# Seven half-size products in place of eight for the gate and up projections of two feed-forwards

## The chip, the core and the metric

The kernel runs on one core of a Trainium2 chip. The metric is the device time of one execution in microseconds, the median of several runs. Inputs and outputs are fp32. Engines are named as in the profile: PE is TensorE's matmul, PEld its weight load, DVE VectorE, ACT ScalarE, POOL GpSimd, SP the engine that issues the DMAs.

## What is computed

Two layers of a first block, each a mixer of four kinds of heads and a feed-forward, and then two attention layers of a second block, over 512 tokens of width 1024. The change touches the two feed-forwards alone. Of one, the reference computes (h is the normalised x):

```python
def conv_glu_ffn(h, w_gate, w_up, conv_w, w_down):
    gate = causal_dwconv(h @ w_gate, conv_w)      # 3 taps along the tokens, per column
    return (jax.nn.gelu(gate, approximate=True) * (h @ w_up)) @ w_down
# w_gate, w_up: 1024 x 2816; w_down: 2816 x 1024
# x = x + rms_norm(conv_glu_ffn(rms_norm(x, pre_ffn_g[l]), ...), post_ffn_g[l])
```

## The kernel before

**Precision.** A product in fp32 is made of three matmuls in fp32r: each operand is split into hi (a cast on ScalarE) and lo = source - hi (a subtraction on VectorE, or on GpSimd where eng says so); `mm3` issues hi x hi, hi x lo and lo x hi into the same PSUM tile.

**Weights.** `wload` takes a buffer wr (two of them, 4 KB a partition each), loads 512 KB from HBM by SP, and splits it into wh and wl (four buffers each). `preload` does the same for a view that comes later.

**Gate and up.** A feed-forward has NF = 22 tiles f of 128 columns of w_gate and as many of w_up. For each, `fm` runs 8 blocks of 128 rows x 3 matmuls = 24 matmuls of 512 columns (the tokens) into one PSUM tile psA. Behind each f: a scaled copy out of PSUM on ScalarE, two steps of the convolution on VectorE (gate read from PSUM), a gelu on ScalarE, the multiplication by the up tile, and the split of the result, which stays in SBUF in the form that the down projection reads. The first three tiles run in halves of 256 tokens (`fm_first`), so that they can start on tokens 0 to 255 while the norm of the others is still made. `next_norm` normalises the four blocks of 128 tokens as the projection before delivers them, and `trans_split` transposes each in 8 transposes and splits it out of PSUM.

**Down.** `out_proj` multiplies the activations by w_down, in two halves of 512 columns; a step is two f: 4 token blocks x 2 x 3 = 24 matmuls of 512 columns, into four PSUM tiles. Then `residual_norm` makes the norm and adds x. `then` names the weights that are preloaded before the last of these.

**Order.** Program order is not the order on the engines. Every instruction goes into a planner (`Plan`), which simulates the five engines with costs written in it, gives out instructions by their rank in program order as they become ready and as buffers are free, and then emits one static order; each engine runs its instructions in that order. wr, wh and wl are taken strictly in turn. In the planner's costs the engines do not slow one another.

Every instruction is recorded at one line (L328, the helper that hands it to the planner), so rows are told apart by tiles: psA, psS and psD are the PSUM pools; p4h, p4p and p4w are pools of 4 KB tiles with 8, 8 and 16 buffers; p is a pool of ten 2 KB tiles; st are small ones; xd is x in HBM.

## Time and profile before

| | before |
|---|---|
| median of 3 runs | 2045.97 us (2045.56 to 2046.21) |
| profiled execution | 2043.82 us, span 2042.0 us |
| TensorE busy | 96% of the span |
| VectorE, ScalarE, GpSimd busy | 62%, 47%, 17% |
| TensorE's granted clock, mean | 0.989 |
| DMA | 94 GB/s mean |

The span goes from the first to the last instruction. Busy shares are averages over stages with different limits, so what an engine is worth has to be read from the windows of a stage. A row of a timeline merges neighbouring instructions of one kind; its duration then reaches from the first start to the last end. Spans of GpSimd are rough, so the ends of instructions on other engines beside them are the better measure.

### The profile page before, as it was taken

The numbers are of one execution on the slowest core, as the hardware profiler recorded it, in microseconds if no ns is written. First come the engines' busy times: TensorE is split into PE (matmuls) and PEld (weight loads), VectorE is DVE, ScalarE is ACT, GpSimd is POOL, SyncE is SP. The second block draws the span as 40 slices with busy tenths as digits, with TensorE's granted clock in tenths as the row PEclk, the third lists the DMA queues.
The fourth block names the chain that finished last, engine by engine and source line by source line (L and its number), as shares of the span: only waits on it lengthen the run. The fifth ranks groups of instructions, "written<-read, shape, count | busy, mean of one in ns | idle before, by whom it ended". The sixth has DMA issues, their size and how long they took to land.

```text
span 2042.0 us, 33217 instructions
## 1 busy us (share of the span) xinstructions
PE 1963.9 (96%) x13254; PEld 1663.4 (81%) x13254; DVE 1265.9 (62%) x2313; ACT 955.0 (47%) x1721; POOL 356.8 (17%) x403
## 2 busy tenths in 40 slices
PE   6999999999999999999999999999999999999999
PEld 5888778888888878787788888888899988888787
DVE  7697883644442266879836444422548886558796
ACT  5763363433332246633634333322446663457782
POOL 3312121100000023112203000000323331105131
PEclk9999999999999999999999999999999999999999
DMA  5321224433332433301344333325331213331121
GB/s 159 99 71 36 71 67 164 117 100 93 94 102 93 155 108 93 76 23 55 94 150 119 93 94 102 93 93 175 114 83 49 77 62 114 126 91 53 62 73 62
DMA packets 231305, 191.88 MB, mean 94 GB/s; under 512 B 22224, under 2 KB 201072, under 8 KB 231152
## 3 DMA queue, kind: packets, MB, share of 16 engines
q1 hardware_dynamic: 231152, 189.77, 30.4%
q8 instruction: 104, 1.70, 0.4%
q14 instruction: 49, 0.40, 0.1%
HBM read 174.54 MB, written 15.20 MB: 93 GB/s over the span
## 4 chain that ended last, share of the span: by engine, by line
PE 80%; DVE 11%; ACT 3%; issue 2%; POOL 2%; DMA 1%; SPq 1%; DVEq 0%; ACTq 0%; POOLq 0%
PE psA L328 59%; PE psS L328 12%; PE psD L328 9%; DVE p4w L328 7%; DVE wl L328 1%; POOL st L328 1%; DVE p L328 1%; DVE st L328 1%; ACT p4w L328 1%; DVE p4p L328 1%; SPq L328 1%; ACT wh L328 1%; DVE p4h L328 0%; DMA p4p<-in_x_dram 0%; ACT p L328 0%
## 5 line engine op out<-in xcount | busy, mean ns | idle before, releaser
L328 PE MATMUL psA<-p4h,wh 128*128 128x512 f32 (+1 forms) x2144 | 626.0, 376 | 4.0 <-ACT p4h L328 2.6
L328 DVE TENSOR_TENSOR wl<-wr,wh 128x1024 fp32r<-128x1024 f32 (+5 forms) x290 | 336.6, 1165 | 392.2 <-ACT wh L328 386.8
L328 ACT CAST wh<-wr 128x1024 fp32r<-128x1024 f32 (+6 forms) x304 | 299.0, 990 | 474.8 <-PE psA L328 283.8
L328 PEld LDWEIGHTS psA<-p4h,wh 128*128 128x128 f32 x2144 | 392.6, 190 | 83.2 <-ACT p4h L328 4.4
L328 PE MATMUL psA<-p4h,wl 128*128 128x512 f32 (+1 forms) x1072 | 403.2, 377 | 1.5 <-DVE wl L328 1.5
L328 PE MATMUL psA<-wh,p4h 128*128 128x256 f32 (+1 forms) x1792 | 353.0, 290 | 2.1 <-DVE p4h L328 1.7
L328 PEld LDWEIGHTS psA<-wh,p4h 128*128 128x128 f32 x1792 | 284.0, 190 | 6.6 <-DVE p4h L328 2.3
L328 PE MATMUL psA<-wl,p4h 128*128 128x256 f32 (+1 forms) x896 | 259.8, 290 | 0.0
L328 POOL TENSOR_SCALAR st<-st 128x1 f32<-128x1 f32 (+4 forms) x108 | 40.0, 370 | 1139.1 <-ACT p4w L328 781.4
L328 PEld LDWEIGHTS psA<-p4h,wl 128*128 128x128 f32 x1072 | 203.9, 190 | 35.5 <-DVE wl L328 1.7
L328 PEld LDWEIGHTS psA<-wl,p4h 128*128 128x128 f32 x896 | 170.5, 190 | 1.6
L328 PE MATMUL psA<-wh,p4w 128*128 128x512 f32 (+1 forms) x540 | 159.5, 368 | 0.0
L328 ACT ACTIVATE p<-p 128x512 f32<-128x512 f32 (+2 forms) x174 | 88.1, 526 | 107.1 <-DVE p L328 105.9
L328 POOL TENSOR_TENSOR st<-st,c 128x1 f32<-128x1 f32 (+4 forms) x106 | 113.9, 1077 | 7.5
L328 PEld LDWEIGHTS psA<-wh,p4w 128*128 128x128 f32 x540 | 96.5, 188 | 18.4 <-issue 0.7
L328 ACT ACTIVATE p4w<-psA 128x256 f32<-128x256 f32 (+5 forms) x138 | 61.6, 451 | 101.9 <-PE psA L328 100.9
L328 PE MATMUL psS<-p4w,p4w 128*64 128x64 f32 (+9 forms) x800 | 98.1, 283 | 7.4 <-DVE p4w L328 7.3
L328 PE MATMUL psS<-consts,p4w 128*128 128x128 f32 (+1 forms) x448 | 71.0, 293 | 34.4 <-DVE p4w L328 18.8
L328 PE MATMUL psA<-wl,p4w 128*128 128x512 f32 (+1 forms) x270 | 98.4, 365 | 0.0
L328 PE MATMUL psS<-wh,p4w 128*128 128x512 f32 x300 | 97.4, 395 | 0.0
L328 DVE TENSOR_TENSOR p<-psA,p 128x512 f32<-128x512 f32 x54 | 37.3, 690 | 95.7 <-PE psA L328 94.2
L328 PEld LDWEIGHTS psS<-consts,p4w 128*128 128x128 f32 x448 | 55.1, 154 | 44.4 <-DVE p4w L328 17.1
(228 smaller groups left out, 3242.5 us busy)
## 6 DMA issues: line engine op xcount, KB each, us to landing
wr<-in_w_in_dram SPq DMA_DIRECT2D x44, 512.0 KB, 3.8
wr<-in_ffn_w_gate_dram SPq DMA_DIRECT2D x44, 512.0 KB, 3.8
wr<-in_ffn_w_up_dram SPq DMA_DIRECT2D x44, 512.0 KB, 3.9
wr<-in_ffn_w_down_dram SPq DMA_DIRECT2D x44, 512.0 KB, 3.5
wr<-in_w_out_dram SPq DMA_DIRECT2D x16, 512.0 KB, 4.4
wr<-in_a_w_in_dram SPq DMA_DIRECT2D x16, 512.0 KB, 3.8
wr<-in_b_w_in_dram SPq DMA_DIRECT2D x16, 512.0 KB, 3.9
p4w<-xd SPq DMA_DIRECT2D x12, 512.0 KB, 4.8
```

The lines of the kernel that those rows point to most:

```text
L328: op.fn(*op.args, **op.kw)
```

## The change

For 256 columns (p) of w_gate or w_up, called one n, the weights are seen as 2 x 2 blocks B of 512 rows x 128 columns, the activations as 2 x 2 blocks A of 256 tokens x 512 rows, and the four products of 256 tokens x 128 columns are put together from seven block products in place of eight (Winograd's form). The sums of blocks of activations (s1 to s4) are made once in each feed-forward, in `norm_blocks`, by VectorE and GpSimd before the transposes, and are then transposed and split as blocks of their own. The sums of blocks of weights (t1 to t4) are made for every n by `seven_weights`, in three stages that the loop calls one n ahead: both halves of the raw weights sit in the two wr buffers; GpSimd subtracts (four times 128x512, two of them in place in wr); ScalarE and VectorE split. A product is 12 matmuls of 256 columns. The seven products are added up by VectorE out of PSUM into an SBUF tile u; the convolution and the gelu work on that tile, and GpSimd multiplies by the up half. The activations are kept in fp32 and split later, by `lhs`, while the down projection runs. The lead-in (`lead`) prepares all of the first n and the first stage of the second before the feed-forward begins. PSUM pools of the projection before are used in another order.

```diff
         return h, rest
 
+    def trans4(self, src, blk, t):
+        ps = self.ps("S")
+        for k in range(4):
+            self.tr(ps[:, k * 128:(k + 1) * 128], src[:, k * 128:(k + 1) * 128])
+        self.split(*(b[:, :, t * 128:(t + 1) * 128] for b in blk), ps.rearrange("p (k n) -> p k n", k=4))
+    def norm_blocks(self, steps, grow):
+        gb = self.bcast_row(grow, D)
+        blk, xns = {}, []
+        lo, hi = slice(0, 512), slice(512, 1024)
+        def put(key, src, t, tag):
+            if key not in blk:
+                blk[key] = [self.p4([128, 4, 256], F32R, tag) for _ in range(2)]
+            self.trans4(src, blk[key], t)
+        for t, _ in enumerate(steps):
+            xn = self.p4()
+            self.norm_tok(self.xt[t], gb, xn)
+            xns.append(xn)
+            if t >= 2:
+                put("a11", xns[t - 2][:, lo], t - 2, "h")
+                put("a12", xns[t - 2][:, hi], t - 2, "h")
+        def rest():
+            for j in range(2):
+                x, y = xns[j], xns[2 + j]
+                s1, s2, s3, s4 = (self.p2() for _ in range(4))
+                self.add(s1, y[:, lo], y[:, hi])
+                self.sub(s2, s1, x[:, lo])
+                self.sub(s3, x[:, lo], y[:, lo], self.G)
+                self.sub(s4, x[:, hi], s2)
+                put("s2", s2, j, "p")
+                put("s1", s1, j, "h")
+                put("s3", s3, j, "p")
+                put("s4", s4, j, "p")
+                put("a22", y[:, hi], j, "h")
+        return blk, rest
+    def seven_weights(self, W, c0, out):
+        raw = [self.new(self.pwr, 2, [128, 4, 256], F32, "wr", "wr") for _ in range(2)]
+        for i in range(2):
+            self.SP.dma_start(out=raw[i], in_=self.cols(W, c0, 256)[:, i * 4:i * 4 + 4])
+        b = [[raw[i][:, :, j * 128:(j + 1) * 128] for j in range(2)] for i in range(2)]
+        pair = lambda: [self.new(p, 4, [128, 2, 4, 128], F32R, tag, tag) for p, tag in ((self.pwh, "wh"), (self.pwl, "wl"))]
+        hi, lo = pair()
+        for i in range(2):
+            self.split(hi[:, i], lo[:, i], b[i][0], eng=self.G if out.get("pool") else None)
+        out["b11"], out["b21"] = ((hi[:, i], lo[:, i]) for i in range(2))
+        yield
+        hi, lo = pair()
+        t = self.p4([128, 2, 4, 128])
+        self.sub(t[:, 1], b[0][1], b[0][0], self.G)
+        self.sub(t[:, 0], b[1][1], t[:, 1], self.G)
+        self.split(hi, lo, t)
+        out["t2"], out["t1"] = ((hi[:, i], lo[:, i]) for i in range(2))
+        self.sub(b[1][0], b[1][0], t[:, 0], self.G)
+        self.sub(b[0][1], b[1][1], b[0][1], self.G)
+        yield
+        hi, lo = pair()
+        d = self.p4([128, 2, 4, 128], F32R, "p")
+        self.split(hi[:, 0], lo[:, 0], b[0][1])
+        self.split(hi[:, 1], lo[:, 1], b[1][1])
+        self.split(d[:, 0], d[:, 1], b[1][0], eng=out.get("eng"))
+        out["t3"], out["b22"] = ((hi[:, i], lo[:, i]) for i in range(2))
+        out["t4"] = d[:, 0], d[:, 1]
+        yield
+    def product(self, ps, blk, w):
+        for k in range(4):
+            self.mm3(ps, (w[0][:, k, :], w[1][:, k, :]), (blk[0][:, k, :], blk[1][:, k, :]), k == 0, k == 3)
     def hp(self, h, k, c0, c1):
         return h[0][k // 2][:, k % 2, c0:c1], h[1][k // 2][:, k % 2, c0:c1]
 
@@ -1853,46 +1931,102 @@
             for n, w in hold:
                 part(ps1, t, n, w)
             if t == NT - 1:
-                self.preload(*then, eng=self.G)
+                then() if callable(then) else self.preload(*then, eng=self.G)
             done(t, [ps0[t], ps1[t]])
             yield t
 
-    def ffn_views(self, l):
+    def ffn_weights(self, l):
         I = self.I
-        return [self.cols(I[k][l], f * 128, 128) for f in range(NF) for k in ("ffn_w_gate", "ffn_w_up")]
-
-    def ffn(self, l, h, rest, then):
+        outs = [{"eng": (self.G, None)[n % 2]} for n in range(NF)]
+        gens = [self.seven_weights(I[k][l], p * 256, outs[2 * p + i]) for p in range(NF // 2)
+                for i, k in enumerate(("ffn_w_gate", "ffn_w_up"))]
+        def lead():
+            outs[0]["pool"] = True
+            for i in (0, 0, 0, 1):
+                next(gens[i])
+        return outs, gens, lead
+    def ffn(self, l, blk, rest, weights, then):
 
         I = self.I
         Wd = I["ffn_w_down"][l]
-        views = self.ffn_views(l) + [self.out_rows(Wd, 0, 0)]
-        acts = []
-        first = self.fm_first(h, [self.wload(v) for v in views[:3]], rest)
-        self.preload(views[3])
-
-        def proj(i):
-            if i < 3:
-                return first[i]
-            w = self.wload(views[i])
-            self.preload(views[i + 1])
-            return self.fm(h, w)
-
-        for f in range(NF):
-            psg, psu = proj(2 * f), proj(2 * f + 1)
-            c = self.p2()
-            self.act(c, psg, AF.Copy, scale=self.fcols[l](f, 2))
-            for j in (1, 0):
-                s = 2 - j
-                self.stt(c[:, s:], psg[:, :S - s], self.fcols[l](f, j), c[:, s:], ALU.mult, ALU.add)
-            self.act(c, c, AF.Gelu_apprx_tanh)
-            self.mul(c, psu, c)
-            a = self.p4([128, 2, S], F32R, "w" if f < 16 else "p")
-            self.split(a[:, 0, :], a[:, 1, :], c)
-            acts.append(a)
-        gb = self.bcast_row(I["post_ffn_g"][l], D)
-        self.xt = self.load_x(acts[NF - 1][:, 0, :].bitcast(F32), "w")
-        return self.out_proj(Wd, lambda k, t: (acts[k][:, 0, t * 128:(t + 1) * 128], acts[k][:, 1, t * 128:(t + 1) * 128]),
-                             list(range(0, NF, 2)), lambda t, ps: self.residual_norm(t, ps, gb, "w"),
+        outs, gens, _ = weights
+        acts, tiles, conv = [], {}, []
+        lo, hi = slice(0, 256), slice(256, 512)
+        def head(n):
+            w, u = outs[n], self.p4([128, 4, 256])
+            ps = self.ps("A")
+            self.product(ps[:, lo], blk["a11"], w["b11"])
+            self.product(ps[:, hi], blk["a12"], w["b21"])
+            self.act(u[:, 3], ps[:, lo], AF.Copy)
+            self.add(u[:, 0], ps[:, hi], u[:, 3])
+            tiles[n] = u
+        def more(n):
+            if n < len(gens):
+                next(gens[n])
+            elif n == NF:
+                self.preload(self.out_rows(Wd, 0, 0))
+        head(0)
+        head(1)
+        rest()
+        for n in range(NF):
+            if n >= 2:
+                head(n)
+            w, u = outs[n], tiles.pop(n)
+            more(n + 1)
+            ps = self.ps("D")
+            self.product(ps[:, lo], blk["s2"], w["t2"])
+            self.add(u[:, 3], ps[:, lo], u[:, 3])
+            ps = self.ps("S")
+            self.product(ps[:, hi], blk["s1"], w["t1"])
+            if n + 1 < NF:
+                more(n + 1)
+            self.product(ps[:, lo], blk["s3"], w["t3"])
+            two = lambda a: a.rearrange("p (a n) -> p a n", a=2)
+            self.add(u[:, 1:3], two(ps), u[:, 3:4].broadcast_to([128, 2, 256]))
+            self.add(u[:, 3], ps[:, hi], u[:, 1])
+            ps = self.ps("A")
+            self.product(ps[:, hi], blk["s4"], w["b22"])
+            if n + 2 < NF:
+                more(n + 2)
+            self.product(ps[:, lo], blk["a22"], w["t4"])
+            self.add(u[:, 1:3], two(ps), u[:, 1:3])
+            if n % 2 == 0:
+                conv = []
+                for i in range(2):
+                    g = u[:, 2 * i:2 * i + 2].rearrange("p a n -> p (a n)")
+                    c = self.p2()
+                    conv.append(c)
+                    self.act(c, g, AF.Copy, scale=self.fcols[l](n + i, 2))
+                    for j in (1, 0):
+                        s = 2 - j
+                        self.stt(c[:, s:], g[:, :S - s], self.fcols[l](n + i, j), c[:, s:], ALU.mult, ALU.add)
+                    self.act(c, c, AF.Gelu_apprx_tanh)
+                continue
+            u = u.rearrange("p (f a) n -> p f (a n)", f=2)
+            for i in range(2):
+                self.mul(u[:, i], u[:, i], conv[i], self.G)
+            acts.append(u)
+        gb = self.bcast_row(I["post_ffn_g"][l], D, "p")
+        parts, self.xt = {}, None
+        def lhs(k, t):
+            for p in range(k // 2, min(k // 2 + 2, NF // 2)):
+                if p not in parts:
+                    parts[p] = [self.p4([128, 2, S], F32R, tag) for tag in ("h" if p < 7 else "p", "w")]
+                    self.split(*parts[p], acts[p])
+            if (k, t) == (NF - 1, NT - 1) and not self.xt:
+                self.xt = self.load_x(parts[k // 2][1][:, 0, :].bitcast(F32), "w")
+            return tuple(a[:, k % 2, t * 128:(t + 1) * 128] for a in parts[k // 2])
+        return self.out_proj(Wd, lhs, list(range(0, NF, 2)), lambda t, ps: self.residual_norm(t, ps, gb, "w"),
                              "SSSD", "AAAD", then)
 
     def layer1(self, l, steps):
@@ -1912,17 +2046,18 @@
         mla = self.mla_items(l, W, h, TC)
         mem = self.mem_items(l)
         self.merge(self.project(gdn + gate_d + hgrn + gla + mla + gate_a + gate_b + mem))
+        weights = self.ffn_weights(l)
         gb = self.bcast_row(I["post_mix_g"][l], D)
         mt = self.mixT
         self.xt = self.load_x(mt[3][:, 0, :].bitcast(F32), "p")
         steps = self.out_proj(Wo, lambda k, t: (mt[k][:, 0, t * 128:(t + 1) * 128], mt[k][:, 1, t * 128:(t + 1) * 128]),
-                              order, lambda t, ps: self.residual_norm(t, ps, gb, "p"), "AAAD", "SSSD",
-                              self.ffn_views(l)[:3])
+                              order, lambda t, ps: self.residual_norm(t, ps, gb, "p"), "DAAA", "DSSS",
+                              weights[2])
         if self.upto == f"mix{l}":
             return run(steps)
-        h, rest = self.next_norm(steps, I["pre_ffn_g"][l], "h")
+        blk, rest = self.norm_blocks(steps, I["pre_ffn_g"][l])
         then = self.gdn_views(1, I["w_in"][1])[:2] if l == 0 else self.a_views()
-        return self.ffn(l, h, rest, then)
+        return self.ffn(l, blk, rest, weights, then)
 
 
```

## Rows read from the trace of the kernel before

**Rows 1.** The page: busy us (share of the span) xinstructions.
```profile
PE 1963.9 (96%) x13254; PEld 1663.4 (81%) x13254; DVE 1265.9 (62%) x2313; ACT 955.0 (47%) x1721; POOL 356.8 (17%) x403
```

**Rows 2.** Busy us by windows: PE, PEld, DVE, ACT, POOL, granted clock, DMA, GB/s.
```profile
400.00:450.00 50.00, 50.00 (x220) 41.03 (x219) 24.49 (x29) 18.13 (x24) 0.00 (x0) 1.00 0.33 95
650.00:700.00 50.00, 50.00 (x216) 40.29 (x215) 12.48 (x14) 10.12 (x11) 0.19 (x1) 1.00 0.47 157
...
366.74:370.99 4.25, 4.25 (x21) 4.25 (x21) 4.25 (x6) 2.00 (x2) 1.55 (x1) 0.50 0.73 185
```

**Rows 3.** The chain that ended last, feed-forwards: start, duration, what.
```profile
379.29 233.63 PE psA L328 x1053
612.93 4.20 PE psS L328 x18
617.13 1.40 PE psD L328 x6
```

**Rows 4.** Timeline of VectorE, 1st and 18th: start, duration, instruction [idle before].
```profile
404.29 0.69 DVE L328 TENSOR_TENSOR p<-psA,p 128x512 f32<-128x512 f32 x1 [2.05 <-PE psA L328]
...
591.06 0.69 DVE L328 TENSOR_TENSOR p<-psA,p 128x512 f32<-128x512 f32 x1 [2.04 <-PE psA L328]
```

**Rows 5.** Timeline of TensorE at a feed-forward's start.
```profile
363.92 0.73 PE L328 MATMUL psS<-consts,p4w 128*128 128x128 f32 x4 [3.81 <-DVE p4h L328]
...
377.49 1.04 PE L328 MATMUL psS<-consts,p4w 128*128 128x128 f32 x8
...
379.87 0.28 PE L328 MATMUL psA<-p4h,wl 128*128 128x256 f32 x1
...
381.99 0.28 PE L328 MATMUL psA<-p4h,wl 128*128 128x256 f32 x1
```

**Rows 6.** Timeline of VectorE and GpSimd where both work: early, and before a feed-forward.
```profile
19.36 2.17 POOL L328 TENSOR_SCALAR p<-consts 128x512 f32<-128x512 f32 x1
20.09 1.64 DVE L328 SCALAR_TENSOR_TENSOR p4w<-p4p,st,p4w 128x1024 f32<-128x1024 f32 x1
...
352.27 1.28 DVE L328 TENSOR_TENSOR p4p<-p4p,p4p 128x512 f32<-128x512 f32 x2
...
357.42 2.40 POOL L328 TENSOR_TENSOR wl<-wr,wh 128x1024 fp32r<-128x1024 f32 x1
358.09 0.74 DVE L328 SCALAR_TENSOR_TENSOR p4p<-psS,st,p4w 128x512 f32<-128x512 f32 x1
358.75 1.62 DVE L328 TENSOR_TENSOR p4p<-p4p,p4p 128x512 f32<-128x512 f32 x1
359.77 2.79 POOL L328 TENSOR_TENSOR wl<-wr,wh 128x1024 fp32r<-128x1024 f32 x1
360.29 2.82 DVE L328 TENSOR_TENSOR p4p<-p4p,p4p 128x512 f32<-128x512 f32 x1
```

**Rows 7.** Groups by form, 410 to 590 us: count | busy us, mean ns | idle before.
```profile
L328 DVE TENSOR_TENSOR wl<-wr,wh 128x1024 fp32r<-128x1024 f32 x33 | 40.4, 1225 | 63.7 <-ACT wh L328 62.2
L328 ACT CAST wh<-wr 128x1024 fp32r<-128x1024 f32 x33 | 34.7, 1052 | 81.5 <-PE psA L328 81.5
...
L328 DVE TENSOR_TENSOR p<-psA,p 128x512 f32<-128x512 f32 x16 | 11.1, 691 | 32.7 <-PE psA L328 32.7
...
L328 DVE TENSOR_TENSOR p4w<-p,p4w 128x512 fp32r<-128x512 f32 x13 | 8.9, 683 | 0.0
L328 ACT ACTIVATE p4w<-p 128x512 fp32r<-128x512 f32 x13 | 8.2, 633 | 0.0
```

**Rows 8.** Instructions on wr, 136.5 to 139 us: issue ns, starts, landing.
```profile
L328 SPq DMA_DIRECT2D wr<-in_w_in_dram x2: 395/404/413, 137.2 to 137.7; - x2
...
DMA to landing us min/median/max: 3.4/3.6/3.9
```

**Rows 9.** Timeline of VectorE at the same start.
```profile
376.02 1.28 DVE L328 SCALAR_TENSOR_TENSOR p4w<-p4p,st,p4w 128x1024 f32<-128x1024 f32 x1
377.21 0.42 DVE L328 TENSOR_TENSOR p4h<-psS,p4h 128x256 fp32r<-128x256 f32 x1
```

## The prediction

> **What bounds the kernel now.** I read the page first, then the windows of a feed-forward, then the chain that ended last, then the groups by form, and at the end single pieces of the timeline. The page shows TensorE at 96% of the span and GpSimd at 17% [rows 1]. In a feed-forward TensorE is busy for the whole of each window at the full granted clock, VectorE for about half of it, and GpSimd does next to nothing [rows 2]. The chain agrees: one unbroken TensorE piece of 233.63 us is the gate and up projections of the first layer, and behind it comes the down projection in steps of 4.20 us [rows 3]; the second layer repeats it. So in this stretch nothing but fewer or shorter matmuls can save time, as long as the other engines keep up, and the reader should look for the engine that would not.
>
> The pace of today: the first and the last of 18 multiplications by an up tile start at 404.29 and 591.06 us [rows 4], 17 periods of 10.99 us. A period is one f (a gate and an up tile of 128 columns), 48 matmuls of 512 columns at 229 ns. I call "one n" what the change works on at a time: 256 columns of one of the two matrices, which cost the same 48 matmuls, 10.99 us. There are 22 n in a layer and 44 in all.
>
> **TensorE's share.** An n becomes seven products of 12 matmuls with 256 columns: 84. The trace has such matmuls in the first three projections: at full clock a wl matmul, every third one, stands at 379.87 and another at 381.99, 18 matmuls later [rows 5], so 118 ns each and 1.41 us a product. An n is then 7 x 1.41 = 9.89 us. The gain offered is 1.10 us an n, 48 us in all. Seven eighths would offer more; 256 columns cost slightly over half of 512.
>
> **VectorE and GpSimd, and the port between them.** The weights of an n, two raw halves of 512 KB, now go through four subtractions of 128x512 on GpSimd, a split of 1024 elements and five of 512 (hi on ScalarE, lo = source - hi). The last of these lo parts is on GpSimd for every second n. Each second n also has two products of 128x512 on GpSimd. These now run all through a stretch where GpSimd was idle, and the trace shows what it does to VectorE. An addition p4p<-p4p,p4p with both inputs in SBUF takes 0.64 us (two in 1.28). Issued at 358.75 while GpSimd ran a wl subtraction, it took 1.62 and ended 0.55 after it. The next one, issued at 360.29 under GpSimd's second, took 2.82 and again ended just behind it [rows 6]. GpSimd's second took 2.79 where the first took 2.40: it had waited for VectorE. The scalar_tensor_tensor just before, with one input in PSUM, was not drawn out, 0.74. One with both inputs in SBUF suffers too: 1.64 at 20.09, behind a GpSimd instruction. So an instruction of VectorE with two SBUF inputs and one of GpSimd take turns, whole instruction by whole instruction.
>
> The Trainium skill says so too ("SBUF — State Buffer", section "SBUF: two separate sides"): the pair of ports that both engines share is a lock, and the later one waits for the end of the other's instruction. By that rule the two engines' durations add up; if they shared a rate instead, the additions at 358.75 and 360.29 would have been slowed by the same factor rather than ended where GpSimd did. The trace sides with the rule; without it the second rival below, 2043 us, would be the forecast.
>
> The durations, as the time the port is taken: GpSimd 128x512 is at least 1.07 (the two additions that waited ended at 360.37 and 363.11, 2.74 apart; less one addition's 0.60 leaves 2.14 for 1024), at most 1.20 (half of 2.40) [rows 6]. I take the middle, 1.13. VectorE: 0.60 for 512 (1.28 less the 0.68 that one shows), 1.15 for 1024 (1.225 recorded [rows 7], less the same 0.08), about 0.65 for a scalar_tensor_tensor of 512 from SBUF (a 1024 one shows 1.28 [rows 9], 0.05 over a subtraction).
>
> For two n (one gate, one up):
> - GpSimd: 8 subtractions, 1 lo part, 2 products: 11 x 1.13 = 12.4 us (11.8 to 13.2).
> - VectorE with two SBUF inputs: 9 lo parts of 512 (5.4), 2 of 1024 (2.3), and the 4 convolution steps (2.6), which now read the assembled tile in SBUF where they read PSUM: 10.3 us.
> - Sum on the port 22.7 us (22.1 to 23.5), that is 11.35 an n. TensorE wants 9.89 and the kernel before takes 10.99.
>
> VectorE's additions from PSUM (3 of 256 at 0.42 and 2 of 512 at 0.69 an n [rows 7, 9]) and ScalarE's casts (4.2 us an n from 0.63 and 1.05 [rows 7]) don't take the port; both engines alone would fit (VectorE 15.5 and ScalarE about 12 us for two n).
>
> **The raw buffers.** wr has two buffers, and both halves of one n fill them; before, each held a whole tile's weights and came free after one cast and one subtraction. SP issues the next load when that subtraction ends. Now a half is held until the last splits that read it. From the landing of the second half, in turns on the port: subtraction 1.13, lo of b21 0.60, subtraction 1.13 (it overwrites b21), lo of t 1.15, subtraction 1.13, lo of b22 0.60, lo of t4 1.13 or 0.60, lo of t3 0.60: 7.2 us, 0.3 for hand-overs. Two loads of weights issued 0.5 apart landed 3.4 and 3.9 us after their issue [rows 8]: 4.4 us to the second. Round trip 11.9 us. In the 4.4 us of loading the port is free for the convolution and the products, 2.4 us an n. VectorE's 2.6 us of PSUM additions fall between the links; for an eighth of them to delay one I add 0.3. One n then takes 12.2 us: 1.2 above today, 44 x 1.2 = +53 us. TensorE then idles 2.3 us an n. Bounds: a perfectly packed port, 11.05 (44 x 0.06 = +3 us); half the PSUM additions and the other port work in the way, 13.4 (+106 us).
>
> **Start of a feed-forward, twice.** Before, TensorE stood 3.81 us at 363.92 [rows 5], then ran matmuls of 256 columns at half clock (granted 0.50, 21 records in 4.25 us, some 0.21 each, against 0.118 [rows 2]). Half-width products of three tiles covered the wait for the last tokens, whose normalisation ended at 377.30 [rows 9]. After, only two heads (4 products, 5.65 us) cover it, and the first other product needs s2, made of all four tokens: two sums, a transpose, a split, hence about 4 us behind 377.3. Transposes go from 32 to 56 (24 x 0.13 from 8 in 1.04 [rows 5] = 3 us), splits with them. Per layer I take +6 us: idle 8 us, part of it paid back since the weights of one n run ahead meanwhile; between 0 and 12. Together +12 us.
>
> **Costed at nothing.** The splits of the activations move to the down projection: ScalarE 1.05 and VectorE 1.23 for a pair of f, with as much again for weights, in 5.6 us of matmuls ([rows 3]: a step of 4.20 and 1.40 behind it). VectorE is a quarter busy there [rows 2]; uncovered they would cost up to 25 us a layer. The x reload, now gated by the last split, still has the second half of the down projection, 11 x 5.6 us, before it is used, against 4 us or so for a load. The prefetched weights ahead of the feed-forward take 7 x 1.13 us of GpSimd where three wl subtractions took about 7.6 (two of them in [rows 6]). That is even.
>
> **The sum** against the profiled execution (span 2042.0, time 2043.82): 2043.8 + 53 + 12 = 2109. The median of the runs shown lies 2.2 above that execution, so 2111 us.
>
> **The rivals.**
> - *TensorE stays the bound.* 44 x 9.89, start +12: 2046 - 48 + 12 = 2010 us (2000 to 2025). For it speaks that today's stretch is unbroken; against it, the port sum is above even today's period. It decides if the sum for two n is under 19.8 us; with VectorE's 10.3 that means 0.86 us of port for a GpSimd 512, under the smallest reading, 1.07. This is the case on the other side. Chance 0.15.
> - *The turns cost little, the buffers bind alone.* GpSimd's four subtractions 4.5, a cast and a lo part 1.3, load 4.4: 10.2 to 10.9 an n, -34 to -4 us, with the start 2024 to 2054; about 2043. It needs VectorE's instructions to fall where GpSimd idles; GpSimd's duty of over half speaks against it. Chance 0.08.
> - *The clock falls as well.* TensorE would idle 2.3 us an n. In the trace a stop of 3.81 us was followed by half clock, 1.2 GHz in place of 2.4, until at least 371.0 [rows 2, 5], 7 us. That costs 3.5 us of matmuls, 1.2 more than the slack; if every n had one, 44 x 1.2 = +53 us: 2164. [...] Chance 0.10.
> - *Forecast* (port and buffers, 11.05 to 13.4 an n): 2058 to 2165, chance 0.67.
>
> **Numbers.** 0.2% (4 us) is about what a measurement of this kernel can tell from no change. Faster: 0.15 and half of the second rival, 0.19. Same: 0.04. Slower: 0.77. The range goes from 2022, which leaves out nearly all of the first rival (0.13), to 2165, which leaves out 0.07 above. The forecast's own range is 2058 to 2165.
>
> **What would show it.** Right: the chain in the feed-forward no longer one piece of TensorE, but GpSimd or VectorE pieces on wr, wl and the subtractions; TensorE 80 to 85% busy in its windows; GpSimd 128x512 instructions with spans well above 1.2 us; VectorE lo parts of 512 well above 0.68; about 24.4 us from one gate-and-up pair of n to the next. Wrong: TensorE still at 100% there with 19.8 us for two n, and lo parts at 0.68. The prediction fails if the two engines' instructions hardly meet, or if the loads come much sooner than I think.

## The result and the profile after

The changed kernel takes 2171.24 us (median of 4 runs, 2169.29 to 2174.04) against 2045.76 (4 runs, 2041.9 to 2046.21): 1.062 times as long, 95% interval 1.060 to 1.0637. The profiled execution took 2174.04 us, its span is 2172.3 us, the mean granted clock 0.969. So the sign came true, and of the mechanism the turns and the round trip; the overlap that the forecast counted on did not. +125 us stand where +65 were forecast, 6 us above the range.

The page's busy line, to be read beside [rows 1]: TensorE's share fell from 96 to 92%, VectorE gained 298 us and GpSimd 386.

```profile
PE 1988.0 (92%) x14742; PEld 1740.5 (80%) x14742; DVE 1564.2 (72%) x2631; ACT 1052.3 (48%) x1915; POOL 743.1 (34%) x647
```

Windows of the first feed-forward, columns as in [rows 2]: two of the gate and up projections, one of the down projection.

```profile
500.00:520.00 20.00, 15.92 (x115) 15.31 (x116) 16.67 (x19) 9.24 (x15) 11.43 (x8) 0.91 0.18 54
...
580.00:600.00 20.00, 15.81 (x123) 14.62 (x123) 17.64 (x19) 10.23 (x17) 12.28 (x8) 1.00 0.17 53
...
700.00:720.00 20.00, 20.00 (x87) 16.12 (x86) 5.26 (x5) 4.20 (x4) 0.00 (x0) 1.00 0.58 204
```

TensorE, busy throughout before, now stands for a fifth of these two windows (38.8 of 240 us from 420 to 660 us); no other engine is busy throughout. The down projection is as before. The pace is best read where SP issues the loads of w_gate, once for two n (start, duration, what); these are the third and the eleventh, the last, of the first layer.

```profile
425.27 1.57 SPq L328 DMA_DIRECT2D wr<-in_ffn_w_gate_dram  x2
...
640.47 2.12 SPq L328 DMA_DIRECT2D wr<-in_ffn_w_gate_dram  x2
```

Eight periods in 215.2 us: 26.9 us for two n, 13.45 an n, against the 10.99 of [rows 4] and the 12.2 forecast. In the second layer the same eight take 213.4 us (1217.17 to 1430.57), 13.34 an n. For 44 n that is +106 us. In the first layer the way from the second part of the mixer's output projection (336.39 before, 341.66 after) to the down projection (612.93 [rows 3], and after the change this row of TensorE's timeline) grew from 276.5 to 333.3 us, by 56.8.

```profile
674.98 0.64 PE L328 MATMUL psS<-wh,p4h 128*128 128x512 f32 x2
```

Of these 22 x 2.46 = 54.1 are the pace, and 2.7 are left for the start and the end of the loop (forecast 6). In the second layer the same way grew from 276.3 (1060.55 to 1336.84) to 329.3 us (1133.96 to 1463.28), by 53.0, with 1.3 left. The span grew by 130.3 us, so 20.5 lie outside these two stretches: 5.3 ahead of the first, 11.4 between the two (the first down projection and the second mixer), 3.9 behind.

What the two engines do to each other, in the groups by form from 420 to 660 us:

```profile
L328 DVE TENSOR_TENSOR wl<-wr,wh 128x512 fp32r<-128x512 f32 x72 | 88.3, 1245 | 15.7 <-ACT wh L328 15.7
L328 DVE SCALAR_TENSOR_TENSOR p<-p4w,cols,p 128x511 f32<-128x511 f32 x18 | 27.0, 1541 | 0.5 <-ACT p L328 0.5
...
L328 DVE TENSOR_TENSOR p4w<-psS,p4w 128x256 f32<-128x256 f32 x19 | 8.0, 423 | 0.5
...
L328 POOL TENSOR_TENSOR wr<-wr,p4w 128x512 f32<-128x512 f32 x18 | 35.5, 1973 | 4.2 <-DVE wl L328 4.2
L328 POOL TENSOR_TENSOR p4w<-p4w,p 128x512 f32<-128x512 f32 x18 | 28.3, 1573 | 0.0
```

A lo part of 512 lasts 1245 ns where [rows 7] show 683, a convolution step 1541; the additions out of PSUM keep their 0.42 [rows 9]. A piece of the timeline with both engines, at the end of an even n:

```profile
516.36 2.14 POOL L328 TENSOR_TENSOR wr<-wr,p4w 128x512 f32<-128x512 f32 x1 [0.70 <-DVE wl L328]
517.27 3.48 DVE L328 TENSOR_TENSOR wl<-wr,wh 128x512 fp32r<-128x512 f32 x2
518.46 1.74 POOL L328 TENSOR_TENSOR p4w<-p4w,p 128x512 f32<-128x512 f32 x1
...
520.17 1.74 POOL L328 TENSOR_TENSOR p4p<-wr,p4p 128x512 fp32r<-128x512 f32 x1
```

GpSimd starts an instruction every 1.71 us (518.46, 520.17) and the two lo parts end behind its own. Taking 0.60 for the lo part, 1.11 is left for GpSimd's 512 (forecast 1.13). The turns are as forecast. But the instruction at 518.46 is one of the products, and it stands ahead of the t4 part at 520.17 for which the raw buffer waits.

The chain that ended last, over this even n and the odd n behind it:

```profile
507.68 3.79 PE psS L328 x22
...
514.72 1.50 DVE wl L328
...
521.94 3.88 DMA wr<-in_ffn_w_up_dram
...
525.84 0.64 ACT wh L328
...
526.51 1.27 DVE wl L328
527.78 4.05 DVE p L328 x3
531.83 1.15 DVE wl L328
```

In the even n the chain comes through TensorE: its products feed an addition out of PSUM that stands ahead of the lo part at 514.72 in VectorE's order. In the odd n it is load, cast, lo part, and then 4.05 us of three convolution steps before the next lo part. The reader should hold this against the prediction's sentence that they run while the port is free for loading. Of four convolution steps and two products for two n, one each ran during a load (issued at 506.48 and 507.68; at 519.08 and 521.94):

```profile
507.58 0.74 DVE L328 SCALAR_TENSOR_TENSOR p<-p4w,cols,p 128x510 f32<-128x510 f32 x1
...
521.87 1.29 POOL L328 TENSOR_TENSOR p4w<-p4w,p 128x512 f32<-128x512 f32 x1
```

### The profile page after: what moved, and what is told of

Read it like the earlier page. It is cut to its first block, busy times and chain, and to the rows that moved or that the text cites. A ratio compares the mean times of both kernels' runs of the same rounds, so it can differ in the third digit from the quotient of the medians.

```text
span 2172.3 us, 37134 instructions
## 1 busy us (share of the span) xinstructions
PE 1988.0 (92%) x14742; PEld 1740.5 (80%) x14742; DVE 1564.2 (72%) x2631; ACT 1052.3 (48%) x1915; POOL 743.1 (34%) x647
## 4 chain that ended last, share of the span: by engine, by line
PE 53%; DVE 23%; POOL 7%; DMA 6%; issue 6%; ACT 5%; SPq 0%; DVEq 0%; POOLq 0%; ACTq 0%
PE psA L328 33%; PE psS L328 12%; PE psD L328 9%; DVE p4w L328 9%; DVE wl L328 6%; DVE p L328 5%; DMA wr<-in_ffn_w_up_dram 3%; POOL p4w L328 2%; POOL st L328 2%; DMA wr<-in_ffn_w_gate_dram 2%; DVE p4p L328 2%; ACT p4w L328 2%; ACT wh L328 1%; POOL p4p L328 1%; DVE st L328 1%
## 5 line engine op out<-in xcount | busy, mean ns | idle before, releaser
L328 DVE TENSOR_TENSOR wl<-wr,wh 128x512 fp32r<-128x512 f32 (+4 forms) x380 | 442.7, 1177 | 271.8 <-ACT wh L328 270.7
L328 PE MATMUL psA<-wh,p4h 128*128 128x256 f32 (+2 forms) x1876 | 392.5, 298 | 2.9 <-DVE p4h L328 2.9
L328 ACT CAST wh<-wr 128x1024 fp32r<-128x1024 f32 (+3 forms) x216 | 205.9, 965 | 277.9 <-PE psD L328 114.4
L328 PE MATMUL psA<-p4h,wh 128*128 128x256 f32 (+1 forms) x1344 | 317.8, 327 | 8.1 <-DVE p4h L328 4.5
L328 PE MATMUL psA<-wl,p4h 128*128 128x256 f32 (+2 forms) x980 | 295.4, 302 | 0.7 <-POOL wl L328 0.7
L328 PE MATMUL psA<-p4h,wl 128*128 128x256 f32 (+1 forms) x672 | 223.9, 334 | 37.8 <-DVE wl L328 37.1
L328 PEld LDWEIGHTS psA<-p4h,wh 128*128 128x128 f32 x1344 | 225.3, 193 | 32.0 <-DVE p4h L328 5.0
L328 ACT ACTIVATE wh<-wr 128x512 fp32r<-128x512 f32 x176 | 106.1, 627 | 194.0 <-DMA wr<-in_ffn_w_up_dram 117.3
L328 PE MATMUL psA<-p4p,wh 128*128 128x256 f32 (+1 forms) x576 | 140.0, 329 | 6.8 <-ACT wh L328 6.8
L328 DVE SCALAR_TENSOR_TENSOR p<-p4w,cols,p 128x511 f32<-128x511 f32 (+1 forms) x88 | 99.7, 1177 | 0.9 <-ACT p L328 0.9
```

Of the source, the lines that this page charges most:

```text
L328: op.fn(*op.args, **op.kw)
```

## Experiments

The theory: the round trip of the two raw buffers, in turns on the port, sets the pace, and convolution and products lengthen it because they stand in its links. The rivals: the port's sum or VectorE's work alone; a planned order that knows nothing of turns; the clock. Every run is compared with runs of the kernel before on the same chip (2043 to 2046 us). The pace is read from the w_gate issues in the first feed-forward, as above.

**1. TensorE's own time.** The sums and splits of weights are made for the first n alone.

```diff
-        gens = [self.seven_weights(I[k][l], p * 256, outs[2 * p + i]) for p in range(NF // 2)
-                for i, k in enumerate(("ffn_w_gate", "ffn_w_up"))]
+        outs = [{"eng": self.G}] * NF
+        gens = [self.seven_weights(I["ffn_w_gate"][l], 0, outs[0])] + [iter(lambda: 0, 1)] * (NF - 1)
```

> Leaves out the loads, sums and splits of all weights of gate and up but those of the first n of each layer, which serve for every n; the seven products, their additions, the convolution and the two products on GpSimd stay. Every theory in which the weights' preparation binds: TensorE's 9.89 an n, 2171 - 44 x 3.56 = 2014 us, and TensorE at 100% in the feed-forward's windows. A rival in which TensorE or the additions out of PSUM are slower than the rows of before let me think: above 2030.

Measured 2004.14 us (one run). In the window TensorE never stops:

```profile
500.00:540.00 40.00, 40.00 (x353) 40.00 (x352) 15.92 (x28) 6.94 (x13) 6.68 (x6) 1.00 0.00 1
```

The convolutions of successive pairs start 19.20 us apart, 9.60 us an n (forecast 9.89). The seven products are a gain of 41 us if nothing else is in the way (44 x 1.39 = 61 by the pace; the rest goes at the start and the end of the loops); the loss lies in the making of the weights.

**2. The turns, without the change.** In the kernel before, where GpSimd idles in the feed-forward, it is given work on a scratch tile for every f: five multiplications that read SBUF, or eleven fills that only write it.

```diff
+            fill = self.p2()
+            self.G.memset(fill, 1.0)
+            for _ in range(5):
+                self.mul(fill, fill, fill, self.G)
```

> The kernel before, with work added that nothing waits for: in each f of the feed-forwards GpSimd fills a scratch tile of 128x512 once and multiplies it by itself five times, about 6 us of 10.99. Turns of whole instructions (my theory): VectorE's weight subtractions (two inputs in SBUF, 1225 ns before) and lo parts (683 ns) that meet a multiplication end with it, so means of 1.5 to 1.9 us and 0.9 to 1.3 us, while the convolution steps with one input in PSUM stay at 0.74 to 0.75; the time stays at 2040 to 2052 us, since VectorE is busy for half of that stretch only. A rate that is shared: all three grow by a like factor. No contention: nothing grows.

> The same with eleven fills of the scratch tile for each f and no multiplication, so that GpSimd is busy for as long but reads nothing from SBUF. If it is the reading by GpSimd that takes turns with VectorE's second SBUF input: the weight subtractions stay at 1.2 us. If any work of GpSimd does: as with the multiplications. Time 2040 to 2052 us by both.

Measured 2112.74 and 2063.49 us (one run each), both above what was expected: nothing holds the fillers back, so the planner put them into GpSimd's queue from the first microsecond on, and the long stretch of gate and up began at 446.03 and 387.00 us where it began at 379.29 before [rows 3]. The question is answered by the groups, 410 to 590 us, of the reads:

```profile
L328 DVE TENSOR_TENSOR wl<-wr,wh 128x1024 fp32r<-128x1024 f32 x28 | 40.7, 1455 | 40.8 <-ACT wh L328 39.7
...
L328 DVE TENSOR_TENSOR p4w<-p,p4w 128x512 fp32r<-128x512 f32 x13 | 15.8, 1214 | 0.0
...
L328 DVE SCALAR_TENSOR_TENSOR p<-psA,cols,p 128x510 f32<-128x510 f32 x13 | 9.7, 747 | 0.4
```

and of the writes:

```profile
L328 DVE TENSOR_TENSOR wl<-wr,wh 128x1024 fp32r<-128x1024 f32 x33 | 40.7, 1235 | 59.8 <-ACT wh L328 58.2
...
L328 DVE TENSOR_TENSOR p4w<-p,p4w 128x512 fp32r<-128x512 f32 x14 | 9.6, 684 | 0.0
```

Beside GpSimd's reads the lo part goes from 683 ns [rows 7] to 1214, while the convolution step with one input in PSUM stays at 747, so it is not a rate that all share; beside its writes the lo part stays at 684. The Trainium skill ("SBUF — State Buffer", section "Who interferes with whom") says the same: an instruction of VectorE with two SBUF inputs contends with one of GpSimd that reads SBUF, not with one that only writes it. TensorE's stretch stayed unbroken in both, 235.68 and 234.39 us where it was 233.63 [rows 3], so the turns alone cost that kernel next to nothing there; they cost where someone waits for the weights.

**3. No GpSimd.** Sums of weights, t4 part and products on VectorE.

```diff
-        self.sub(t[:, 1], b[0][1], b[0][0], self.G)
+        self.sub(t[:, 1], b[0][1], b[0][0])
...
-        outs = [{"eng": (self.G, None)[n % 2]} for n in range(NF)]
+        outs = [{"eng": None} for n in range(NF)]
...
-                self.mul(u[:, i], u[:, i], conv[i], self.G)
+                self.mul(u[:, i], u[:, i], conv[i])
```

> The eleven GpSimd instructions for two n (the weight subtractions, one lo part, the two products with the up half) are given to VectorE; all else as in the changed kernel, which takes 13.45 us an n (26.9 for two n, from the starts of the gate loads) and 2171 us. My theory, turns between VectorE and GpSimd inside a round trip through the two raw buffers: a turn of GpSimd costs 1.1 us of the port (1.70 from one VectorE end to the next, less 0.60), the same work on VectorE 0.60, so the round trip loses about 5 x 0.5 us and the waits between turns; VectorE alone is then at 22.1 us for two n, 11.05 an n. Expected 11.3 to 12.4 an n, 2075 to 2125 us, and lo parts of 512 back at 0.68. Rival, VectorE has simply too much to do (it is 80 to 85% busy in the changed kernel, and gets 6.6 us more for two n): no gain or a loss, 2171 or more.

Measured 2073.74 us (2 runs, ratio 1.014, 1.0089 to 1.0195). The window:

```profile
500.00:540.00 40.00, 38.55 (x307) 36.57 (x306) 39.55 (x66) 21.65 (x35) 0.00 (x0) 1.00 0.29 88
```

All the work on one engine is 98 us faster than shared by two, a little better than expected (10.9 us an n in place of 11.3 or more). Lo parts are back at 684 ns, and the pace is 21.8 us for two n, which is now simply VectorE's work (39.55 of 40). The pace is no slower than that of the kernel before (21.98), yet the kernel is: from the last load of the mixer's output weights to the first matmul of the down projection it takes 289.6 and 290.9 us in the two layers, against 285.2 and 285.0. So 10 us of the 25.5 by which its span is longer lie there, and 15 in other stages.

**4. The buffers.** The raw halves of the n numbered 3, 5 to 15 go into tiles of the pool p4w, so that two n can be on their way; alone and with experiment 3.

```diff
-        raw = [self.new(self.pwr, 2, [128, 4, 256], F32, "wr", "wr") for _ in range(2)]
+        raw = [self.p4([128, 4, 256]) if out.get("w") else self.new(self.pwr, 2, [128, 4, 256], F32, "wr", "wr") for _ in range(2)]
...
+        for n in range(3, 16, 2):
+            outs[n]["w"] = True
```

> For n = 3, 5, ... 15 of each feed-forward the raw weights lie in two tiles of the pool w in place of the two raw buffers, so that the loads of one n no longer wait for the splits of the n before; the work is the same. My theory (turns and buffers together): from n = 2 to 16 the load of 4 to 5 us leaves the round trip, and the port's sum of 11.35 an n, or a bit more, is what is left there: 14 n x 2 layers x (13.45 - 11.7) = 49 us less, 2122 us (2100 to 2145). Rival A, the turns cost nothing and the buffers alone bind: those n fall to TensorE's 9.89, 28 x 3.56 = 100 us less, 2071. Rival B, the port alone binds: the loads don't matter, 2165 to 2175.

> Both edits together: VectorE does all, and the raw weights of n = 3, 5, ... 15 lie in tiles of their own. My theory: in the n with four raw buffers VectorE's own 22.1 us for two n bind, 11.05 to 11.5 an n; the others as with VectorE alone. About 10 to 25 us under the kernel with VectorE alone: 2060 to 2105. Rival A (the buffers alone bind): the n in question fall to 9.89 as in the kernel with four raw buffers, so the two are equal.

Measured 2141.47 us (1.0473, 1.0442 to 1.0503) and 2070.51 (1.0126, 1.009 to 1.0162), 2 runs each. The first is 30 us under the changed kernel: the round trip was a limit, but not the only one. Its waits from 460 to 640 us (who waits <- for whom: total us, times, longest) name VectorE's lo parts now:

```profile
POOL p4w L328 <- DVE wl L328: 24.3, 5, 6.5
...
PE psD L328 <- DVE wl L328: 22.0, 9, 6.3
```

The second missed its expectation: 3 us less than experiment 3, which the spread of two runs each does not resolve, in place of 10 to 25. With the loads out of the way VectorE's 21.4 us of work are left.

**5. Convolution and products left out.**

```diff
-                    for j in (1, 0):
-                        s = 2 - j
-                        self.stt(c[:, s:], g[:, :S - s], self.fcols[l](n + i, j), c[:, s:], ALU.mult, ALU.add)
...
-            for i in range(2):
-                self.mul(u[:, i], u[:, i], conv[i], self.G)
```

> Leaves out of the changed kernel the convolution steps on VectorE (four for two n) and the two products with the up half on GpSimd; weights, loads, seven products and their additions stay. My prediction let both run for nothing while the raw weights load, and came to 12.2 us an n; the changed kernel takes 13.45. Theory 1, they fell into the chain of turns instead: without them 11.9 to 12.3 an n, 2171 - 44 x 1.35 = 2112 us (2095 to 2125). Theory 2, the load and the hand-overs were longer than I took them and the convolution and products cost nothing: 13.2 to 13.45, 2160 to 2171.

Measured 2111.74 us (2 runs, 1.0323, 1.0293 to 1.0353), 24.0 us for two n. Its chain shows the round trip bare; first the even n, then the odd one:

```profile
495.57 4.94 DMA wr<-in_ffn_w_gate_dram
...
500.64 1.29 POOL p4w L328
501.93 0.60 POOL wr L328
...
503.59 2.29 POOL wr L328
...
506.62 1.57 POOL p4p L328
...
508.20 4.60 DMA wr<-in_ffn_w_up_dram
...
515.34 3.96 DVE wl L328 x3
519.30 0.60 DVE p4p L328
...
519.93 4.63 DMA wr<-in_ffn_w_gate_dram
```

From landing to the next issue 7.7 us (500.51 to 508.20) and 7.1 (512.80 to 519.93), with loads of 4.6 to 4.9: that is the forecast's 7.5 and 4.4. The changed kernel's links took 9.4 (512.56 to 521.94). So the convolution and the products cost 1.45 us an n, or something that goes with them: this run also had the clock at 1.00 where the changed kernel shows 0.91 in three of the five windows of 20 us from 500 to 600.

**6. The clock alone, the order alone.** 12 matmuls more in every n, where TensorE stands; and convolution and products behind the weights of the next n in program order.

```diff
             ps = self.ps("D")
+            self.product(ps[:, lo], blk["a11"], w["b11"])
             self.product(ps[:, lo], blk["s2"], w["t2"])
```

```diff
             if n + 1 < NF:
                 more(n + 1)
+            if tails:
+                tails.pop()()
...
+            def tail(n=n, u=u):
...
+            tails.append(tail)
```

> The changed kernel with 12 matmuls more in every n: the product of a11 and b11 once more, into the PSUM tile that the product of s2 and t2 then overwrites, so the output stays and TensorE has 1.4 us of work in the place where it stands and waits for the parts of t2. In the changed kernel a stop of 2.34 us there was followed by a granted clock of 0.50. Theory C (the falls of the clock lie on the path of the raw buffers through VectorE's waits for sums in PSUM): the clock stays at 1.00 and the pace goes from 26.9 to 25.5 us or less for two n, 2130 to 2155 us. Theory O (the order of VectorE and GpSimd alone sets the pace): the clock rises, the pace stays, 2165 to 2180 us.

> The changed kernel with the convolution, the gelu and the products of an n put later in program order, behind the last splits of the weights of the n after it: they then rank behind the chain that gives the raw buffers back and can fall into the time of loading. Nothing is left out. Theory O (the static order puts the convolution and the products between the links of the chain): about the 24.0 to 24.8 us for two n of the run that left them out, 2110 to 2130 us. Theory C (the clock is the rest of the cost): under 1 us less for two n, 2150 to 2172 us.

> Both of the last two edits. Theory O: as the run with the later convolution alone, 2110 to 2130 us. Theory C: as the run with the filled stop alone. If both cost something, 10 to 30 us below the better of the two.

Measured 2162.01, 2159.86 and 2155.28 us (3 runs each; 1.0573, 1.0568 and 1.0542, each within 0.0021). With the fill the granted clock is 1.00 in all windows from 440 to 600 us and the pace 26.3: the clock costs about 0.3 us an n, 9 us in all, between the two theories. The second run tested nothing: the planner started the steps as soon as VectorE had nothing ready, and they stand where they stood, between two lo parts:

```profile
496.98 1.28 DVE L328 TENSOR_TENSOR wl<-wr,wh 128x512 fp32r<-128x512 f32 x1 [0.56 <-ACT wh L328]
498.19 4.12 DVE L328 SCALAR_TENSOR_TENSOR p<-p4w,cols,p 128x511 f32<-128x511 f32 x3
502.23 1.22 DVE L328 TENSOR_TENSOR wl<-p4w,wh 128x1024 fp32r<-128x1024 f32 x1
```

The 11 us that it gained lie in other stages: between the two points of experiment 3 it takes 341.7 and 338.1 us, the changed kernel 342.2 and 338.2. So the run with both edits, 5 us lower still, says nothing of the order either.

**7. The order forced.** Besides, in the plan they may not start before the last split of those weights; alone and with the fill.

```diff
+        if self.behind is not None:
+            preds[self.behind] = None
...
             if tails:
+                self.plan.behind = len(self.plan.ops) - 1
                 tails.pop()()
+                self.plan.behind = None
```

> The changed kernel with the convolution, the gelu and the products not only later in program order (which the planner answered by starting them as soon as VectorE had nothing ready, between the same links), but held in the plan behind the last split of the weights of that n. Now four subtractions and the lo parts of an n follow one another with nothing of the convolution between them, and convolution and products stand where the port waits for the next load. Nothing is left out. Theory O: 24.0 to 24.8 us for two n, 2105 to 2130 us. Theory P (the port's sum and the turns cost the same wherever the convolution stands): 26 to 27 us for two n, 2150 to 2175 us.

> The same with the 12 matmuls more in every n that kept the clock at 1.00. Theory O: up to 10 us less than the run beside it where that one's clock falls, the same where it does not. Theory P: 2150 to 2160 us.

Measured 2149.73 and 2154.81 us (3 runs each; 1.0516, 1.0496 to 1.0537, and 1.0532, 1.0507 to 1.0557): by the time at theory P (0.3 us under its range, and in it), by the pace of 25.7 and 25.8 us for two n between the theories. The timeline (the helper's line is L330 here) shows what moved and what did not:

```profile
515.57 2.73 DVE L330 SCALAR_TENSOR_TENSOR p<-p4w,cols,p 128x511 f32<-128x511 f32 x4
...
524.75 3.48 DVE L330 TENSOR_TENSOR wl<-wr,wh 128x512 fp32r<-128x512 f32 x2
528.16 1.78 DVE L330 TENSOR_TENSOR p4p<-wr,p4p 128x512 fp32r<-128x512 f32 x1
```

```profile
525.93 3.45 POOL L330 TENSOR_TENSOR p4w<-p4w,p 128x512 f32<-128x512 f32 x2
```

The four convolution steps now run in 2.73 us while a load is on its way, undisturbed, and the even n gives its buffer back 7.65 us after the landing (507.96 to 515.61). In the odd n the products still take turns with the last lo parts, 9.35 us (520.62 to 529.97), where experiment 5 shows 7.1. So of the 2.9 us for two n that experiment 5 took away, 1.2 were the place of the convolution, and the 1.7 that are left go with the products, by subtraction. With the order forced the fill brings nothing more.

**8. A planner that knows of turns.** In its simulation an instruction of VectorE with two SBUF inputs and one of GpSimd with an SBUF input exclude each other; for the changed kernel and, as a control, for the one before.

```diff
+            sb = sum(not a.tensor.name.startswith("ps") and _free(a) > 1 for a in op.ins)
+            op.turn = op.eng == "POOL" and sb > 0 or op.eng == "DVE" and sb > 1
...
+            if op.turn:
+                start = max(start, port)
+                port = start + op.cost
```

> The changed kernel, with one more rule in the planner: an instruction of VectorE with two SBUF inputs and one of GpSimd with an SBUF input can't run at the same time, so the static order is made for the turns. Theory 1 (the round trip of the two raw buffers in turns and the port's sum bind, and the order adds some because the convolution and the products stand between the links): at best the 12.0 us an n that the run without convolution and products showed, so 2110 to 2150 us. Rival (the order alone was the loss): the port's sum, 11.35 us an n, 2075 to 2095 us. Rival (a greedy planner puts the instructions at the same places with or without the rule): the same 2165 to 2175 us.

> The kernel before with the same rule in the planner, as a control for what the rule does to all other stages. In the feed-forwards GpSimd is idle, so the pace there stays 10.99 us for one f; elsewhere the order changes a little: 2030 to 2055 us by every theory.

Measured 2173.29 us (1.0637, 1.0616 to 1.0658) and 2053.49 (1.005, 1.003 to 1.007), 3 runs each. A planner that takes what is ready gains nothing by knowing: 27.7 us for two n after an earlier start. The control shows that a change of order elsewhere is worth some 10 us by itself.

**9. Products alone on GpSimd.** Experiment 3 with the two multiplications back on GpSimd: as it is, with the rule of experiment 8, with that rule in the gate and up loop only, and this with the raw tiles of experiment 4.

```diff
-                self.mul(u[:, i], u[:, i], conv[i])
+                self.mul(u[:, i], u[:, i], conv[i], self.G)
...
+        self.plan.local = True
         for n in range(NF):
             if n >= 2:
                 head(n)
...
+        self.plan.local = False
         parts, self.xt = {}, None
```

> The kernel with VectorE alone (2072 us, 21.7 us for two n, VectorE 99% busy), but the two products with the up half back on GpSimd as in the change. If GpSimd were free help, VectorE loses 1.2 us for two n: 22 x 1.2 = 26 us less, 2046. By the turns each product takes the port 1.1 us and can hide only behind VectorE's additions out of PSUM: between 10 us less and 20 us more, 2062 to 2092.

> The kernel with the sums of weights on VectorE and only the two products of every second n on GpSimd, planned with the rule of turns. Without the rule it took 2072.6 us, no less than with nothing on GpSimd, although 1.2 us of VectorE's work for two n were gone. Theory 1: VectorE's additions out of PSUM, some 5 us for two n, leave room for the two products; with an order that puts them there VectorE needs 20.5 in place of 21.7 us for two n, 11 x 1.2 x 2 = 26 us less: 2045 to 2060 us, about the kernel before. Rival (each engine runs as it can, and the turns cost what the products save): 2066 to 2076 us.

> The kernel with only the products of every second n on GpSimd, with the rule of turns applied to the gate and up loops alone. Planned with the rule everywhere it took 2059.4 us at about 22.2 us for two n, and the kernel before lost 8 us when the rule was applied to all its stages. Theory (the rule helps in the loop and harms elsewhere): 22.0 to 22.2 us for two n and some 6 to 8 us less, 2050 to 2056 us. Rival (the rule's gain was a change of the feed-forward's start, by a chance of order): 2065 to 2073 us.

> The same, with the raw weights of every second n in tiles of the pool w, so that four raw halves are on their way. VectorE is 95% busy at 22.0 us for two n, that is 21.0 us of work. Theory A (the loads are still awaited at 22.0): 21.0 to 21.4 us for two n, 13 to 20 us less than the run beside it, 2033 to 2043 us, which would be under the kernel before. Theory B (VectorE and the turns bind and the loads only look late): under 5 us less than the run beside it.

Measured 2072.58 us (2 runs, 1.0132, 1.0103 to 1.0161), 2059.41 (3 runs, 1.0081, 1.0061 to 1.0101), 2074.44 (4 runs, 1.0128, 1.0111 to 1.0145) and 2078.02 (4 runs, 1.0147, 1.0129 to 1.0165). The second fell into its range for a wrong reason: its pace is 22.2, not 20.5; its first w_gate issue of the loop came 13 us earlier (381.88 against 394.76). With the rule in the loop alone, expected at 2050 to 2056, that early start is gone, and so is the gain, though the pace of 21.9 is below the 22.4 without the rule. The fourth run, expected at 2033 to 2043 if loads were still awaited, gains nothing either; VectorE is occupied to the last:

```profile
500.00:540.00 40.00, 38.10 (x306) 36.68 (x307) 40.00 (x63) 18.41 (x34) 5.98 (x4) 1.00 0.17 54
```

Its pace is 22.0 where the same raw tiles with the products on VectorE gave 21.4. In this order two products on GpSimd cost VectorE more in turns than their 1.2 us. No version that was tried beats the kernel before.

## Why the prediction was right in direction and short in size

- *TensorE no longer the bound, 9.89 us an n offered.* Right; 9.60 measured, and 16% of standing.
- *Turns, instruction by instruction; 1.13 us for GpSimd.* Right: 1.11, lo parts at 1245 ns, and experiment 2 shows them without the change.
- *Two raw buffers, round trip 11.9 us.* Right: 12.0 in experiment 5, in the links forecast. Experiments 3 and 4 each give back part of the loss by taking away one of the two.
- **The step that failed:** "In the 4.4 us of loading the port is free for the convolution and the products, 2.4 us an n", which put both at nothing. The port was free then, and most of them did not use it: the static order has three of four steps and one of two products between the links, where VectorE has a gap while GpSimd subtracts. The term is 1.45 us an n (13.45 less 12.0), not 0; experiment 7 gives back 0.6 of it by the place of the convolution alone. The pace came out 1.25 us an n longer than forecast in the first layer and 1.14 in the second, 53 of the 65 us by which the profiled execution lies above 2109.
- *Upper bound 13.4 an n, "half the PSUM additions and the other port work in the way".* A wrong sum: 11.9, half of 2.6 and half of 2.4 make 14.4, which is +150 us and 2208 for the end of the range; 13.4 is what 12.2 and half of the 2.4 make. Measured were 13.45 and 13.34: as it was worked out the bound just fails to hold the first layer, as it was worded it holds both.
- *Start +6 us a layer.* 2.7 and 1.3 us beyond the pace, 8 us less than forecast for both.
- *No term for the other stages.* 20.5 us, the second thing that the sum lacks. The planner changed their order too, and the control of experiment 8 shows that this alone can cost 10 us; what cost it here was not traced.
- *Splits at the down projection costed at nothing.* Nearly right: 18 steps take 100.8 us before (612.93 to 713.73) and 101.3 after (674.98 to 776.26); in the second layer TensorE waits another 1.26 us there, at 1465.51, for a lo part of weights that stands behind these splits on VectorE.
- *The clock falls as well* (rival). Half true: it falls in five of the seven pairs of n from 470 to 650 us, and costs 9 us by experiment 6, not 53.
- *24.4 us from pair to pair.* 26.9.

Open: how much of the 1.7 us beside the products could be had back. An order binds each engine by itself: in the odd n GpSimd has nothing behind its last subtraction, so it begins the products at once, while VectorE still has lo parts to make (525.93 and 524.75 in experiment 7). A wait of GpSimd for the last lo part would keep them apart; it wasn't tried. That the products cost the whole 1.7 is a difference of two runs, not a measurement of them alone.

## What to carry to other kernels

Cover has to be in the order, not only in the time: before costing an instruction at nothing because a resource idles for long enough, look which instructions stand before and behind it on its engine, and whether a greedy order will start it in the gaps of the very chain it should keep clear of. When a change moves arithmetic from TensorE to VectorE and GpSimd, price VectorE alone first (21.8 us for two n, against 21.98 before, left nothing to win here), since work on GpSimd that reads SBUF is paid back in turns. Count a buffer's round trip with all that stands between its links. And where a planner orders the whole program, give the stages beside the change a term of their own: here they took 20 of 130 us.

## What was not expected of the hardware

A matmul of 256 columns in an unbroken stretch takes 114 ns (9.60 us for 84), where two starts in the kernel before gave 118 [rows 5]. Fills by GpSimd, which read nothing, took no turn in experiment 2 (684 ns). And the clock fell behind stops shorter than the 3.81 us of [rows 5]: windows of the changed kernel around one that ended at 505.90, with its row in TensorE's timeline,

```profile
505.90 0.39 PE L328 MATMUL psD<-p4p,wl 128*128 128x256 f32 x1 [2.34 <-DVE wl L328]
```

```profile
507.00:509.00 2.00, 2.00 (x12) 2.00 (x11) 1.90 (x5) 0.59 (x1) 0.00 (x0) 0.50 0.63 144
509.00:511.00 2.00, 2.00 (x14) 2.00 (x14) 0.18 (x1) 0.65 (x2) 0.56 (x1) 0.69 1.04 341
511.00:513.00 2.00, 2.00 (x19) 2.00 (x19) 1.46 (x3) 0.47 (x2) 1.07 (x2) 1.00 0.11 40
```

show 0.50 of the full 2.4 GHz, that is 1.2 GHz, soon after a stop of 2.34 us, and the full clock again some 4 us later. The same stop does not always do it. From 470 to 650 us there are seven of 2.33 to 2.35 us, one for two n, and behind those that ended at 477.42 and 587.03 the clock stayed at 1.00:

```profile
587.03 0.39 PE L328 MATMUL psD<-p4p,wl 128*128 128x256 f32 x1 [2.35 <-DVE wl L328]
```

```profile
590.00:595.00 5.00, 5.00 (x46) 5.00 (x44) 3.83 (x6) 1.44 (x4) 2.64 (x3) 1.00 0.46 160
```

What tells the two cases apart stays open.
